# Two encoder layers on one core: a split per conv block, evacuations behind the next block's casts, and projections in two 1024-column chunks

## The chip, the cores and the metric

The kernel runs on one core of one Trainium2 chip. Its time is the device time of one execution in microseconds (us). The time before is the median of three runs. A profiled execution of the same kernel gives the trace; its own time differs a little from that median and stands in the table below.

The engines are named as the profile names them: PE (TensorE, the matrix products; PEld its weight loads), DVE (VectorE), ACT (ScalarE), POOL (GpSimd) and SP (SyncE, which here only issues DMAs).

## The reference, cut to what matters

The input has 256 tokens (two token tiles of 128, called t0 and t1), a model width of 2048 (16 blocks of 128 channels, `kt` 0 to 15) and an inner width of 5632 in the feed-forward part (44 such blocks). There are two layers. Everything is float32.

```python
c_act = jax.nn.silu(c)
for l in range(DEPTH):                       # two layers
    mod = (c_act @ w_mod[l] + b_mod[l]).reshape(bn, 6, d)
    shift_m, scale_m, gate_m = mod[:, 0, None], mod[:, 1, None], mod[:, 2, None]
    shift_f, scale_f, gate_f = mod[:, 3, None], mod[:, 4, None], mod[:, 5, None]

    h = layer_norm(x) * (1.0 + scale_m) + shift_m
    proj = h @ w_in[l]
    uv, q_c, kv_c, k_r, sb, sc, sh, ag = jnp.split(proj, IN_SPLITS, axis=-1)
    y_a = gmlp_mixer(uv, ...)
    y_b = mla_mixer(q_c, kv_c, k_r, ...)
    y_c = short_conv_mixer(sb, sc, sh, ...)
    y_d = conformer_conv(ag, ...)
    y = jnp.concatenate([y_a, y_b, y_c, y_d], axis=-1) @ w_out[l]
    x = layer_norm(ALPHA * x + (1.0 + gate_m) * y, post_mix_g[l], post_mix_b[l])

    h = layer_norm(x) * (1.0 + scale_f) + shift_f
    y = conv_ffn(h, w_up[l], ..., w_down[l])
    x = layer_norm(ALPHA * x + (1.0 + gate_f) * y, post_ffn_g[l], post_ffn_b[l])
```

The weights are read from HBM once each: about 600 MB in the whole run, `w_mod` (the modulation, 2048 x 12288 per layer) among them.

## The kernel before, in words

**Products.** Most products are made of three matrix products in a reduced format: a weight tile `wraw` is split into a rounded part `whi` (a CAST on ACT, L396) and a rest `wlo` (a subtraction on DVE, L397), an activation is split in the same way by `split` (L414: a CAST on ACT at L416, a subtraction on DVE at L417), and PE adds hi x hi, hi x lo and lo x hi. A few products ("exact", tiles `wexact`) take the float32 weight as it is; they need no split, and more time on PE. `splitp` holds four `whi` and four `wlo` tiles of 1024 columns (`wexact` tiles come from the same buffers), and four raw buffers of 1 MB are shared by `wraw`, `wmod` and `gb`. All weight loads are issued by SP in program order, each when its buffer is free.

**The stages**, in order of time: the first input projections of layer 0, done in pieces (`by_pieces`, L1168, fed by `first_mods`, L1428); the rest of the mixers; the output projection, called o0; the up projection with its conv and gate (products `g_c`, `v_c`); the down projection, d0; and the same for layer 1 (o1, d1).

**The modulation** is no stage of its own. A weight unit of 1 MB is loaded (`wmod`) and multiplied and summed along its row by one DVE instruction (L192, or L227 for the gates). `stream` (L338) calls `pump` once per weight unit of the other stages, and a table RATES says how many modulation units that lets in, by stage. What a later step needs and has not been made is made there and then (`need`).

**Stage A, the pieces of layer 0.** A list `turns` sets the order of the pieces: D blocks (the conv branch's columns, one `kt` at a time, four accumulator banks that stay open through the stage) alternate with pieces of U, V, E and B that each take four `kt` at once. Such a piece gets a bank, loads the sum so far into it (`act.copy(o, total)`, L1223), adds its products, and copies the sum out (`act.copy(total, o)`, L1228). Both copies are ACT's. The normalised, modulated activation of one block is `hF`, written by DVE at L1447 when the modulation of that `kt` is known. From `kt` 4 (PLAIN_KT) on, D takes split products and so needs the split activation `hT`. It is made for two blocks at once, after the second block's `hF`:

```python
if kt >= PLAIN_KT and kt % 2 == 1:
    split(hT[kt // 2], hF[kt // 4][:, kt % 4 - 1 : kt % 4 + 1, :])
```

**Output and down projections** (`out_proj`, L601). The 2048 columns are taken in three chunks, of 1024, 512 and 512 columns. A unit of weights is 1 MB: two blocks of 1024 columns, or four of 512, so a unit is always 24 products of 512 columns (or 16 exact ones). Each chunk goes through all blocks (16 for o, 44 for d), with one accumulator bank for each token tile and 512 columns. In o the split activations are kept between chunks; in d there is no room, so each chunk splits all 44 blocks again (instructions `a<-g`, pairs of blocks). When a chunk is done, its banks are evacuated by `finish_bank` (L634): three DVE instructions per bank (`yg` = sum x gate, x update, statistics), queued in `evacs` and popped one per unit of the next chunk. In the last chunk the last four units are held back (`tail`) and done first for t0, then for t1, so that t0's last evacuation and norm (`second`, L667) run while PE still works on t1. t1's last evacuation is ordered behind t0's norm (L641). `gains` loads the norm's gain and bias at the end of the middle chunk.

**Order.** A scheduler places the instructions of each engine, in program order as far as its own cost model likes it; `tc.add_manual_dep(..., order_dep)` pins one instruction behind another of the same engine and adds no wait.

## Time and profile before

| | us |
|---|---|
| median of 3 runs (2260.59 to 2262.27) | 2261.2 |
| profiled execution, its own time | 2257.45 |
| its span, first to last instruction | 2255.7 |
| PE busy | 2198.7 (97%) |
| DVE busy | 1762.5 (78%) |
| ACT busy | 1088.1 (48%) |
| stage A | 0 to about 185 |
| o0 | 307 to 403 |
| d0 | 915 to 1165 |
| o1 | 1411 to 1497 |
| d1 | 2003 to 2244 |

An engine's row of the profile gives its busy time and its share of the span. A row of waits says which instruction group waited for which, the total, how often and the longest. The chain of waits is followed back from the last instruction: each piece is what the next one was released by. A windows row gives, for a stretch, the busy time of PE, PEld, DVE, ACT and POOL with the count of instructions, the granted PE clock, the share of the 16 DMA engines and GB/s. A timeline row gives start, duration, engine, line, operation, output and inputs, and in brackets the idle time ahead of it with what ended it. `L94` is the one line from which all matrix products are issued, so products are told apart by the names of their outputs.

### The profile page before, as it was taken

What the parts mean: (1) busy time and instruction counts of PE and PEld (TensorE: products, weight loads), DVE (VectorE), ACT (ScalarE), POOL (GpSimd) and SP (SyncE); (2) the same over time, 40 slices, a digit from 0 to 9 for tenths busy, and PEclk for the clock granted to TensorE, in tenths of its full rate; (3) what the DMA queues carried; (4) which work ended last, traced back from release to release, by engine and by line L of the source; (5) the groups of instructions that cost most, each with busy time, mean ns of one, the idle gap of its engine ahead of it and who ended that gap; (6) DMA issues with size and microseconds to landing.
All of it is one profiled execution on the core that took longest, in us unless ns stands there. A gap on an engine that the chain in (4) does not pass through costs nothing.

```text
span 2255.7 us, 30853 instructions
## 1 busy us (share of the span) xinstructions
PE 2198.7 (97%) x12128; PEld 1899.5 (84%) x12128; DVE 1762.5 (78%) x2260; ACT 1088.1 (48%) x1617; POOL 28.0 (1%) x49
## 2 busy tenths in 40 slices
PE   7899999899999999999999999999999999999997
PEld 5678886898888888887789899889888888888886
DVE  6779987888888888989876998876765565565676
ACT  4347551454454445544554435444544444454553
POOL 0000000000000000000000000000000000000000
PEclk9999999999999999999999999999999999999999
DMA  9899689687878888898766566765665555555554
GB/s 390 344 370 384 243 337 388 254 313 302 324 290 334 316 333 298 341 348 326 272 240 246 204 226 252 292 227 209 224 255 188 187 187 187 189 195 194 187 188 148
DMA packets 94235, 605.16 MB, mean 268 GB/s; under 512 B 10661, under 2 KB 10853, under 8 KB 28933
## 3 DMA queue, kind: packets, MB, share of 16 engines
q1 hardware_dynamic: 93752, 602.29, 71.7%
q8 instruction: 95, 1.56, 0.3%
q0 software_dynamic: 336, 0.89, 0.1%
q14 instruction: 52, 0.42, 0.0%
HBM read 601.05 MB, written 2.10 MB: 267 GB/s over the span
## 4 chain that ended last, share of the span: by engine, by line
PE 80%; DVE 5%; issue 1%; ACT 1%; DMA 0%; POOL 0%; DVEq 0%; POOLq 0%; ACTq 0%
PE g_c L94 22%; PE v_c L94 22%; PE d L94 19%; PE o L94 7%; PE C_c L94 3%; PE D_c L94 2%; PE U_c L94 1%; DVE wlo L397 1%; PE B_c L94 1%; PE E_c L94 1%; DVE convD L826 1%; DVE wmod L192 0%; PE ps_xT L532 0%; DVE a L417 0%; DMA wraw<-in_w_out_dram 0%
## 5 line engine op out<-in xcount | busy, mean ns | idle before, releaser
L396 ACT CAST whi<-wraw 128x1024 fp32r<-128x1024 f32 (+1 forms) x632 | 644.9, 1044 | 774.0 <-PE g_c L94 209.9
L397 DVE TENSOR_TENSOR wlo<-wraw,whi 128x1024 fp32r<-128x1024 f32 (+1 forms) x632 | 751.6, 1214 | 313.2 <-ACT whi L396 299.4
L94 PE MATMUL d<-whi,a 128*128 128x512 f32 x1344 | 388.2, 390 | 2.0 <-ACT whi L396 2.0
L94 PE MATMUL v_c<-hT,whi 128*128 128x512 f32 (+1 forms) x1456 | 341.5, 383 | 0.0
L94 PE MATMUL g_c<-hT,whi 128*128 128x512 f32 (+1 forms) x1344 | 313.3, 380 | 0.0
L94 PEld LDWEIGHTS v_c<-hT,whi 128*128 128x128 f32 x1456 | 264.6, 189 | 48.0
L192 DVE SCALAR_TENSOR_TENSOR wmod<-wmod,cB 128x2048 f32<-128x2048 f32 x126 | 286.9, 2285 | 17.5 <-DMA wmod<-in_w_mod_turned_dram 17.4
L94 PEld LDWEIGHTS d<-whi,a 128*128 128x128 f32 x1344 | 252.7, 188 | 55.0 <-ACT whi L396 2.8
L94 PEld LDWEIGHTS g_c<-hT,whi 128*128 128x128 f32 x1344 | 243.5, 189 | 43.2
L94 PE MATMUL d<-wlo,a 128*128 128x512 f32 x672 | 234.3, 391 | 4.6 <-DVE wlo L397 4.6
L94 PE MATMUL v_c<-hT,wlo 128*128 128x256 f32 x1400 | 190.2, 283 | 0.0
L94 PEld LDWEIGHTS v_c<-hT,wlo 128*128 128x128 f32 x1400 | 183.1, 191 | 6.5
L94 PE MATMUL g_c<-hT,wlo 128*128 128x256 f32 x1280 | 175.8, 283 | 0.0
L94 PEld LDWEIGHTS g_c<-hT,wlo 128*128 128x128 f32 x1280 | 168.2, 191 | 5.9
L94 PEld LDWEIGHTS d<-wlo,a 128*128 128x128 f32 x672 | 126.5, 188 | 33.8 <-DVE wlo L397 7.6
L227 DVE SCALAR_TENSOR_TENSOR macc<-wmod,cact,macc 128x2048 f32<-128x2048 f32 x60 | 140.7, 2344 | 8.0 <-DMA wmod<-in_w_mod_gates_dram 7.9
L416 ACT CAST a<-g 128x512 fp32r<-128x512 f32 x132 | 80.9, 618 | 72.0 <-PE d L94 70.1
L94 PE MATMUL o<-whi,a 128*128 128x512 f32 x384 | 110.6, 393 | 0.0
L94 PE MATMUL D_c<-hT,whi 128*128 128x256 f32 x432 | 84.6, 296 | 12.1 <-ACT hT L416 11.1
L417 DVE TENSOR_TENSOR a<-g,a 128x512 fp32r<-128x512 f32 x132 | 88.0, 684 | 7.4 <-ACT a L416 7.4
L94 PEld LDWEIGHTS o<-whi,a 128*128 128x128 f32 x384 | 72.0, 188 | 16.3 <-issue 1.2
L94 PEld LDWEIGHTS D_c<-hT,whi 128*128 128x128 f32 x432 | 70.5, 199 | 17.7 <-ACT hT L416 14.4
(345 smaller groups left out, 2525.2 us busy)
## 6 DMA issues: line engine op xcount, KB each, us to landing
wraw<-in_ffn_w_up_dram SPq DMA_DIRECT2D x168, 1024.0 KB, 4.9
wmod<-in_w_mod_turned_dram SPq DMA_DIRECT2D x126, 1024.0 KB, 6.3
wraw<-in_ffn_w_down_dram SPq DMA_DIRECT2D x88, 1024.0 KB, 4.8
wmod<-in_w_mod_gates_dram SPq DMA_DIRECT2D x64, 1024.0 KB, 5.6
wraw<-in_w_in_dram SPq DMA_DIRECT2D x27, 1024.0 KB, 4.9
wraw<-in_w_out_dram SPq DMA_DIRECT2D x26, 1024.0 KB, 6.4
wexact<-in_w_in_dram SPq DMA_DIRECT2D x46, 512.0 KB, 7.8
wexact<-in_ffn_w_up_dram SPq DMA_DIRECT2D x16, 512.0 KB, 8.9
```

What stands on the lines that cost most here:

```text
L94: pe.matmul(o, lhsT, rhs, start=start, stop=stop, skip_group_check=True)
L192: i = dve.scalar_tensor_tensor(out=raw, in0=raw, scalar=1.0, in1=cB[:, k0 : k0 + n], op0=ALU.mult, op1=ALU.mult, accum_out=total)
L227: i = dve.scalar_tensor_tensor(out=acc, in0=w, scalar=col, in1=acc, op0=ALU.mult, op1=ALU.add)
L396: act.copy(hi[:, :m], r)
L397: i = dve.tensor_tensor(out=lo[:, :m], in0=r, in1=hi[:, :m].bitcast(F32), op=ALU.subtract)
L416: act.copy(hi, src)
L417: dve.tensor_tensor(out=lo, in0=src, in1=hi.bitcast(F32), op=ALU.subtract)
L826: dve.scalar_tensor_tensor(out=yd[:, j, 30 - k :], in0=glu[:, j, : S - 30 + k], scalar=CW(k, j), in1=yd[:, j, 30 - k :], op0=ALU.mult, op1 ...
```

## The change

There are four parts, none of which alters what is computed.

1. **Split per block.** `first_mods` splits each block from `kt` 4 on by itself as soon as its `hF` is written, 128 x 256 elements instead of 128 x 512 per instruction, so six pairs become twelve single splits on ACT and on DVE. The CASTs (the activation's, and that of the block's weights) are collected in a table `casts`.
2. **Evacuations behind casts.** In `side`, the copy of a piece's sum out of its bank gets an order dependence behind the CASTs of the next D block, if the next turn is one. The remaining transposes of x are popped at fixed turns.
3. **Two chunks.** Output and down projections take 1024 and 1024 columns. In d each block is split twice instead of three times: 132 `a<-g` instructions become 88 on ACT and on DVE. In o0 six units of the second chunk are exact, as many products as before (eight products of each kind move between two mixers' columns). The tail is done bank by bank for each token tile. The modulation is pumped in the last chunk too, up to five units from its end; the first chunk's gate is fetched ahead of its last products, its evacuations start as each token tile ends, and `gains` runs six units ahead of the end.
4. **Rates.** Layer 0: out 1.3 to 1.53, down 0.83 to 0.7. Layer 1: out 0.6 to 0.65, down 0.7 to 0.6.

Three places show what the instruction order does. First ACT in stage A, around two D blocks (`hT<-hF` and the `whi` behind it are a D block's casts; `sumU<-U` evacuates a piece, `V<-sumV` opens the next). Before:

```order
L1228 COPY sumU<-U_0_650 128x512
L1223 COPY V_0_728<-sumV 128x512
L1228 COPY sumU<-U_1_661 128x512
L1223 COPY V_1_735<-sumV 128x512
L416 CAST hT<-hF_134 128x2x256
L396 CAST whi<-wraw 128x1024
L1228 COPY sumV<-V_0_728 128x512
L1223 COPY E_0_788<-sumE 128x512
```

and now:

```order
L417 CAST hT<-hF_134 128x256
L397 CAST whi<-wraw 128x1024
L1229 COPY sumU<-U_0_640 128x512
L1224 COPY V_0_720<-sumV 128x512
L1229 COPY sumU<-U_1_651 128x512
L1224 COPY V_1_727<-sumV 128x512
L417 CAST hT<-hF_134 128x256
L397 CAST whi<-wraw 128x1024
L1229 COPY sumV<-V_0_720 128x512
```

The casts stood behind both copies of the piece ahead of them; now they stand ahead of both, and every block has its own activation cast.

Second, DVE in d0, before in the second and third chunk (`yg<-d_102400` evacuates the second chunk's bank of t0):

```order
L417 TENSOR_TENSOR a<-g,a 128x2x256 x4
L397 TENSOR_TENSOR wlo<-wraw,whi 128x1024 x2
L192 SCALAR_TENSOR_TENSOR wmod,total<-wmod,cB 128x2048
L417 TENSOR_TENSOR a<-g,a 128x2x256
L205 TENSOR_TENSOR mod_3_12_8698<-total,bcol_104 128x8
L417 TENSOR_TENSOR a<-g,a 128x2x256 x2
L397 TENSOR_TENSOR wlo<-wraw,whi 128x1024 x2
L225 TENSOR_SCALAR macc<-wmod,cact 128x2048
L417 TENSOR_TENSOR a<-g,a 128x2x256
L639 TENSOR_TENSOR yg<-d_102400_8315,gate_5_4778 128x512
```

and now, in the second of two chunks:

```order
L398 TENSOR_TENSOR wlo<-wraw,whi 128x1024 x2
L192 SCALAR_TENSOR_TENSOR wmod,total<-wmod,cB 128x2048
L418 TENSOR_TENSOR a<-g,a 128x2x256
L398 TENSOR_TENSOR wlo<-wraw,whi 128x1024 x2
L418 TENSOR_TENSOR a<-g,a 128x2x256
L192 SCALAR_TENSOR_TENSOR wmod,total<-wmod,cB 128x2048
L398 TENSOR_TENSOR wlo<-wraw,whi 128x1024 x2
L418 TENSOR_TENSOR a<-g,a 128x2x256
L192 SCALAR_TENSOR_TENSOR wmod,total<-wmod,cB 128x2048
L205 TENSOR_TENSOR mod_3_12_8904<-total,bcol_104 128x8
```

Per unit of weights (two `wlo`) there is one `a` in place of two, and the modulation units reach further into the stage.

Third, DVE at the end of d0, where the next stage waits for t0's norm (`x_97` is t0; the rows up to `rs_d0p` are its last evacuation and statistics). Before:

```order
L639 TENSOR_TENSOR yg<-d_153600_8817,gate_5_4778 128x512
L642 SCALAR_TENSOR_TENSOR x_97<-x_97,yg 128x512
L645 BN_STATS st_d_7394<-x_97 128x6
L512 BN_AGGR mv_d0p_9243<-st_d_7394 128x2
L514 TENSOR_SCALAR rs_d0p_9245<-mv_d0p_9243 128x1
```

and now:

```order
L641 TENSOR_TENSOR yg<-d_102400_8310,gate_5_4734 128x512
L641 TENSOR_TENSOR yg<-d_102401_8311,gate_5_4734 128x512
L644 SCALAR_TENSOR_TENSOR x_97<-x_97,yg 128x512 x2
L647 BN_STATS st_d_7406<-x_97 128x6 x2
L514 BN_AGGR mv_d0p_9185<-st_d_7406 128x2
L516 TENSOR_SCALAR rs_d0p_9187<-mv_d0p_9185 128x1
```

Two banks are evacuated ahead of the norm in place of one. The same holds for t1 behind it, and for the ends of o0 and o1. PE's order at these ends has 24 products of t1 for its first bank and 24 for its second behind the last product of t0 in d0, d1 and o1; in o0, where the exact blocks of t1's first bank are mostly done earlier, one exact and 12 split products, and then four exact and 12 split ones.

The diff:

```diff
@@ -33,8 +33,8 @@
 
 
 RATES = [
-    dict(B=1.3, C=1.5, out=1.3, first=1.2, up=0.68, down=0.83),
-    dict(D=0.8, U=0, V=0, B=0.3, C=0.6, E=0.6, out=0.6, up=0.3, down=0.7),
+    dict(B=1.3, C=1.5, out=1.53, first=1.2, up=0.68, down=0.7),
+    dict(D=0.8, U=0, V=0, B=0.3, C=0.6, E=0.6, out=0.65, up=0.3, down=0.6),
 ]
 
@@ -56,9 +56,9 @@
 
 GROUPS = {
     "w_in": ((C_UV, 512), (C_UV + 512, 512), (C_Q, 768), (C_SB, 512), (C_SC, 1024), (C_AG, 1024)),
-    "w_out": ((0, 1024), (1024, 512), (1536, 512)),
+    "w_out": ((0, 1024), (1024, 1024)),
...
-    "ffn_w_down": ((0, 1024), (1024, 512), (1536, 512)),
+    "ffn_w_down": ((0, 1024), (1024, 1024)),
 }
 
 
@@ -356,6 +356,7 @@
             tc.add_manual_dep(i.ins, name, order_dep, reason="the norm is what the next products wait for")
 
     exact_turn = [0]
+    cast = [None]
@@ -393,7 +394,7 @@
                 hi = splitp.tile([P, 1024], F32R, tag="whi", name="whi")
                 lo = splitp.tile([P, 1024], F32R, tag="wlo", name="wlo")
             r = raw[:, k * width : k * width + m]
-            act.copy(hi[:, :m], r)
+            cast[0] = act.copy(hi[:, :m], r)
             i = dve.tensor_tensor(out=lo[:, :m], in0=r, in1=hi[:, :m].bitcast(F32), op=ALU.subtract)
             held(i, "split")
             for j in range(per):
@@ -413,8 +414,9 @@
 
     def split(dst, src):
         hi, lo = dst[:2]
-        act.copy(hi, src)
+        i = act.copy(hi, src)
         dve.tensor_tensor(out=lo, in0=src, in1=hi.bitcast(F32), op=ALU.subtract)
+        return i
 
     def group(w, c0, width, name, then, ntm=0, nk=2, hF=None, bg=0, spare=0, begun=None):
 
@@ -596,7 +598,7 @@
 
         return cps, rest
 
-    CHUNKS = ((0, 1024), (1024, 512), (1536, 512))
+    CHUNKS = ((0, 1024), (1024, 1024))
 
     def out_proj(l, w, src, order, gate_of, name, post_g, post_b, before, then, plain={}, bg=0):
 
@@ -604,25 +606,25 @@
         stats = [new_stats(f"{name}{t}") for t in range(2)]
         box, kept = {}, {}
 
-        def products(t, item, ps, u, nk):
+        def products(t, item, ps, u, nk, banks=None):
...
@@ -726,7 +728,7 @@
             last = c0 + width == D
             nk = 2048 // width
             units = nkt // nk
-            state = {"tail": []}
+            state = {"tail": [], "ps": []}
 
...
@@ -749,42 +751,41 @@
...
-            def unit(item, u, state=state, c0=c0, width=width, nk=nk, last=last, units=units):
-                if u == 0:
-                    state["ps"] = [
-                        [acc_tile(f"{name}_{c0}{t}{i}") for i in range(width // 512)] for t in range(2)
-                    ]
+            def banks_of(t, state=state, c0=c0, width=width):
+                state["ps"].append([acc_tile(f"{name}_{c0}{t}{i}") for i in range(width // 512)])
+
+            def unit(item, u, state=state, c0=c0, nk=nk, last=last, units=units):
                 if last and u >= units - 4:
                     state["tail"].append((item, u))
-                    if evacs:
+                    return
+                if not last and u == units - 1:
+                    box["gate"] = gate_of()
+                for t in range(2):
+                    if u == 0:
+                        banks_of(t)
+                    products(t, item, state["ps"], u, nk)
+                    if not last and u == units - 1:
+                        evacs.extend(lambda t=t, i=i: finish_bank(t, i, state["ps"], c0) for i in range(2))
+                    if last and u == 0 and t == 0:
+                        while len(evacs) > 2:
+                            evacs.pop(0)()
+                if evacs and last and u > 0:
+                    evacs.pop(0)()
+                if last and u == units - 6:
+                    gains()
+
+            for u in range(units):
+                stream(lambda: load(u), lambda item, u=u, unit=unit: unit(item, u), bg, not last or u < units - 5)
+
+            def done(state=state, c0=c0, nk=nk, last=last):
+                if not last:
+                    while len(evacs) > 3:
                         evacs.pop(0)()
                     return
                 for t in range(2):
-                    products(t, item, state["ps"], u, nk)
-                if evacs:
-                    evacs.pop(0)()
-
-            for u in range(units):
-                stream(lambda: load(u), lambda item, u=u, unit=unit: unit(item, u), bg, not last)
-
-            def done(state=state, c0=c0, nk=nk, last=last):
-                if c0 == 0:
-                    box["gate"] = gate_of()
-                if c0 + 512 == D - 512:
-                    gains()
-                for t in range(2):
-                    for item, u in state["tail"]:
-                        products(t, item, state["ps"], u, nk)
-                while evacs:
-                    evacs.pop(0)()
-                if not last:
-                    evacs.extend(
-                        lambda t=t, i=i: finish_bank(t, i, state["ps"], c0)
-                        for t in range(2)
-                        for i in range(len(state["ps"][t]))
-                    )
-                    evacs.pop(0)()
-                    return
+                    for i in range(2):
+                        for item, u in state["tail"]:
+                            products(t, item, state["ps"], u, nk, (i,))
                 if before is not None:
                     before()
                 for t in range(2):
@@ -1216,7 +1217,7 @@
                 else:
                     chan_major([None] * i + [o], kt, part, (2 * i, 2 * i + 1), first, last)
 
-        def side(g, kts):
+        def side(g, kts, before):
             for i, total in enumerate(sums[g]):
                 o = acc_tile(f"{g}{l}_{i}")
                 if kts[0] > 0:
@@ -1225,7 +1226,9 @@
                 if g == "U" and kts[-1] == KT - 1:
                     u_banks.append(o)
                 else:
-                    act.copy(total, o)
+                    i = act.copy(total, o)
+                    for c in before:
+                        tc.add_manual_dep(i.ins, c.ins.name, order_dep, reason="the next conv block is waited for")
...
+                if g == "D" and not exact:
+                    casts[k].append(cast[0])
 
...
-                side(g, kts)
+                g1, k1 = turns[n + 1] if n + 1 < len(turns) else ("", ())
+                side(g, kts, casts.get(k1[0], ()) if g1 == "D" else ())
             if kts[:1] == (LATE_KT,) and g != "D":
                 next(mods)
-            if n > 6 and rest_of_x:
+            if n in (6, 7, 13, 14, 20, 21):
                 rest_of_x.pop(0)()
         mix_v(None, [[x] for x in sums["V"]])
         phase(l, "B")
@@ -1425,6 +1431,8 @@
 
+    casts = {}
+
     def first_mods(hF):
 
         quarter = normed_T(hF)
@@ -1445,8 +1453,8 @@
             x = hF[kt // 4][:, kt % 4, :]
             sc, sh = MOD[(0, SCALE_M, kt)], MOD[(0, SHIFT_M, kt)]
             i = dve.tensor_scalar(out=x, in0=x, scalar1=sc, scalar2=sh, op0=ALU.mult, op1=ALU.add)
-            if kt >= PLAIN_KT and kt % 2 == 1:
-                split(hT[kt // 2], hF[kt // 4][:, kt % 4 - 1 : kt % 4 + 1, :])
+            if kt >= PLAIN_KT:
+                casts[kt] = [split([h[:, kt % 2, :] for h in hT[kt // 2][:2]], x)]
...
-            plain={1024: 2, 1536: 4} if l == 0 else {},
+            plain={1024: 6} if l == 0 else {},
         )
```

More of the change, by code (lines that the diff above doesn't have):

```diff
@@ L611, in products @@
                 sp = (u + 1) * nk == nkt and k == nk - 1
-                n = len(ps[t])
-                cols = [slice(i * 512, (i + 1) * 512) for i in range(n)]
+                banks = banks or range(len(ps[t]))
+                cols = [slice(i * 512, (i + 1) * 512) for i in range(len(ps[t]))]
                 ahi, alo = acts[k]
@@ L616, in products @@
                 if lo is None:
-                    for i in range(n):
+                    for i in banks:
                         mm(ps[t][i], ah, hi[:, cols[i]], st, sp)
                     continue
-                for i in range(n):
+                for i in banks:
                     mm(ps[t][i], ah, hi[:, cols[i]], st, False)
-                for i in range(n):
+                for i in banks:
                     mm(ps[t][i], ah, lo[:, cols[i]], False, False)
                 al = alo[:, t * P : (t + 1) * P]
-                for i in range(n):
+                for i in banks:
                     mm(ps[t][i], al, hi[:, cols[i]], False, sp)
```

## The prediction

> **What bounds the kernel now.** I read the page first, for the share of PE, then what PE waited for, then the stretches in which it waited.
>
> ```profile
> span 2255.7 us, 30853 instructions
> PE 2198.7 (97%) x12128; PEld 1899.5 (84%) x12128; DVE 1762.5 (78%) x2260; ACT 1088.1 (48%) x1617; POOL 28.0 (1%) x49
> ```
>
> PE is busy for all but 57 us of the span, and the change leaves its products as many as they were. So a gain can only come out of those 57 us and out of products that ran at a lower clock. The waits of PE say where they lie:
>
> ```profile
> PE D_c L94 <- ACT hT L416: 11.1, 6, 4.0
> PE ps_xT L532 <- ACT xn L97: 10.0, 4, 5.3
> ...
> PE d L94 <- DVE wlo L397: 4.6, 7, 1.9
> PE d L94 <- ACT whi L396: 2.0, 2, 1.7
> ```
>
> The first row is stage A: the D blocks wait for their split activation. The second is the start of the next stage after a norm. The last two are the down projection. The stretches, with busy time of PE, PEld, DVE, ACT, POOL, then granted clock, DMA share and GB/s:
>
> ```profile
> 60.00:80.00 20.00, 15.86 (x86) 14.35 (x85) 17.05 (x21) 6.67 (x12) 0.00 (x0) 0.83 0.88 333
> 80.00:100.00 20.00, 17.09 (x90) 14.60 (x88) 14.09 (x16) 7.79 (x12) 0.00 (x0) 0.91 0.96 356
> ...
> 186.00:216.00 30.00, 30.00 (x141) 26.41 (x140) 28.68 (x25) 18.29 (x46) 0.39 (x2) 1.00 1.02 413
> ...
> 20.00:186.00 166.00, 151.94 (x805) 126.36 (x806) 116.16 (x132) 75.85 (x123) 4.10 (x7) 0.96 0.93 365
> 307.00:403.00 96.00, 95.92 (x337) 63.09 (x336) 80.61 (x101) 21.71 (x28) 1.60 (x2) 1.00 0.92 352
> 1049.00:1110.00 61.00, 54.43 (x228) 42.13 (x227) 60.21 (x75) 33.54 (x42) 0.00 (x0) 0.99 0.81 297
> 914.60:1164.60 250.00, 243.40 (x1056) 198.19 (x1055) 219.90 (x257) 121.71 (x154) 1.47 (x2) 0.99 0.81 300
> 2002.80:2244.40 241.60, 241.59 (x1065) 199.20 (x1063) 160.89 (x183) 121.91 (x151) 0.92 (x1) 1.00 0.52 184
> ```
>
> In 1049 to 1110, the middle of d0, DVE is busy 60.21 of 61.00 us: there it is the bound. Elsewhere PE is, except in stage A, where no engine is full and the D blocks wait.
>
> **Down projection, layer 0.** The chain of waits gives PE's undisturbed pace:
>
> ```profile
> 914.60 134.68 PE d L94 x594
> ```
>
> 134.68/594 is 0.2267 us per product, so the 1056 products of d0 need 239.4 us; the stretch is 250.0. It loses 10.6 us. What DVE does there per product unit follows from its groups in d0 (914.6 to 1110):
>
> ```profile
> L397 DVE TENSOR_TENSOR wlo<-wraw,whi 128x1024 fp32r<-128x1024 f32 x68 | 80.9, 1220 | 8.6 <-ACT whi L396 7.6
> L192 DVE SCALAR_TENSOR_TENSOR wmod<-wmod,cB 128x2048 f32<-128x2048 f32 x26 | 59.4, 2283 | 0.0
> L417 DVE TENSOR_TENSOR a<-g,a 128x512 fp32r<-128x512 f32 x49 | 32.4, 684 | 4.0 <-ACT a L416 4.0
> ```
>
> A unit of 24 products takes PE 24 x 0.2267 = 5.44 us. In the 512-column chunks DVE had per unit two `wlo` (2.44), two `a` (1.37) and 0.83 modulation units (0.83 x 2.283 = 1.89): 5.70, more than PE. Now it is two `wlo`, one `a` (0.68) and 0.7 units (1.60): 4.72, so 0.72 us per unit are free. The 44 `a` that go are 22 in this stage, 15 us of DVE's 219.9. The number of modulation units pumped in the stage stays (33 x 0.83 = 27.4, 39 x 0.7 = 27.3), and they reach into the end of the last chunk, where DVE had been idle. The cost that stays is the first chunk's evacuation: four banks of three instructions; at the 0.684 of the `a` row of the same width I take 8.2 us, which 0.72 per unit needs 11 units to absorb, while four split tiles hold PE for two units, 10.9 us. So a little may show: I take -9.5 us, between -6 (half of the evacuation shows) and -10.6. Cast of ACT: 22 fewer there, hidden (ACT is busy 121.7 of 250).
>
> d1 has 241.6 us against the same 239.4; at most 2.2 to win. DVE is at 161 there, without modulation; -1, between 0 and -2.2.
>
> **Stage A.** ACT works in order, and the casts stood behind the copies of the piece before. ACT, then DVE, then PE:
>
> ```profile
> 65.24 0.62 ACT L416 CAST hT<-hF 128x512 fp32r<-128x512 f32 x1 [3.45 <-DVE hF L1447]
> ...
> 99.19 0.59 ACT L1228 COPY sumU<-U 128x512 f32<-128x512 f32 x1 [2.25 <-PE U L94]
> 99.81 0.59 ACT L1223 COPY V<-sumV 128x512 f32<-128x512 f32 x1
> 100.33 0.61 ACT L416 CAST hT<-hF 128x512 fp32r<-128x512 f32 x1
> ```
>
> ```profile
> 50.87 0.41 DVE L1447 TENSOR_SCALAR hF<-hF,mod 128x256 f32<-128x256 f32 x1
> ...
> 97.75 0.41 DVE L1447 TENSOR_SCALAR hF<-hF,mod 128x256 f32<-128x256 f32 x1
> ```
>
> ```profile
> 65.91 1.31 PE L94 MATMUL D_c<-hT,whi 128*128 128x256 f32 x2 [3.99 <-ACT hT L416]
> ...
> 84.48 1.92 PE L94 MATMUL D_c<-hT,whi 128*128 128x256 f32 x5 [2.79 <-ACT hT L416]
> ```
>
> The rows show both faults that the change takes up. Block 4 had its `hF` at 51.3, but the cast waited for block 5's and came at 65.24: PE stood 3.99 us. Blocks 8 and 9 had theirs by 98.2, but the cast waited on ACT behind a copy that waits for PE, and came at 100.33. With single splits ahead of the copies these waits (11.1 us over six) can go. The two long ones also lowered the clock: 0.83 of 15.86 busy us and 0.91 of 17.09 are 2.7 and 1.5 us. So the stage can win at most 11.1 + 4.2 = 15.3 us. It will not win all: a faster PE frees buffers earlier, and the loads must follow. The stage moves 166 us x 365 GB/s = 60.6 MB, at 413 (the fullest row) 147 us, so the DMA engines would have to run nearly full throughout to give 15. They also run at 413 right behind, so bytes that come late there cannot be made up. From half of the bound I take -7.5; ends 0 and -15.3. The cost of the twelve half-size casts and subtractions instead of six is covered, ACT being busy 76 of 166 us and DVE 116. The copies now stand behind the casts, which can make a piece's bank free later; that is the last rival.
>
> The Trainium skill, "DMA: Bandwidth & Descriptors", section "Where 436 GB/s comes from", says that for loads from HBM the HBM limit of about 358 GB/s per core binds. By that rule stage A, at 365, has no room, its term is 0 and the time 7.5 us higher. The row of 186 to 216 at 413 disagrees for this core.
>
> **Output projection, layer 0.** The rate 1.53 lets in 11 x 1.53 = 16.8 modulation units instead of 12 x 1.3 = 15.6; SP's order has 11 of them and one more half of exact weights among the first chunk's eight `wraw`, where it had 9. That is 2.5 MB more before the second chunk. At 352 GB/s it is 7.1 us if nothing hides it; the 8% of the 96 us in which the DMA engines were idle are 7.7 us and could hold it. PE was full there, so nothing is won. I take +1, ends 0 and +7.
>
> **The three starts of a next stage.** t0's last evacuation now has two banks, three more DVE instructions: at 0.684 each +2.05 us on the path to the norm. The rows of t0's last `yg` and of the end of its norm, for o0 and for d0:
>
> ```profile
> 392.66 0.69 DVE L639 TENSOR_TENSOR yg<-o,gate 128x512 f32<-128x512 f32 x1 [8.73 <-PE o L94]
> ...
> 397.20 2.29 DVE L192 SCALAR_TENSOR_TENSOR wmod<-wmod,cB 128x2048 f32<-128x2048 f32 x1
> ...
> 407.07 0.16 DVE L700 SCALAR_TENSOR_TENSOR rs_o0r<-m_o,rs_o0r 128x1 f32<-128x1 f32 x1 [0.67 <-POOL rs_o0r L125]
> ```
>
> ```profile
> 1153.73 0.69 DVE L639 TENSOR_TENSOR yg<-d,gate 128x512 f32<-128x512 f32 x1 [2.40 <-PE d L94]
> ...
> 1163.69 0.16 DVE L700 SCALAR_TENSOR_TENSOR rs_d0r<-m_d,rs_d0r 128x1 f32<-128x1 f32 x1 [0.73 <-POOL rs_d0r L125]
> ```
>
> In d0 the path took 10.1 us, and t1's 48 products behind t0 take 10.9, so PE waited almost nothing. With 12.2 it waits: 12.2 - 10.9, about 1 for the cast and transpose, +2.3, and if the idle PE starts at a lower clock, as after the 2.79 us above, +0.5: +2.8, ends +1 and +3.5. In o0 the path took 14.6 us, two modulation units of 2.29 within; PE's last product came 10.2 after t0's (the wait of 5.3 ended about 1 us behind 407.07). Now one unit stands there (-2.3), +2.05, and t1's products after t0's are 24 split ones at 0.2267 and five exact ones at 0.43, 7.6 us in place of 10.2 (+2.6): +2.4, and t1's own evacuation of two banks behind that norm +0.6: +3, ends +1 and +5. The 0.43 is an estimate: o0's 95.92 busy us less 240 split products, over its 96 exact ones. In o1 the wait was about 4 us (the row's total of 10.0 is 5.3 and that, mostly); path 12.2 against 10.9 leaves about 2.5: -1, ends -1.5 and +2. The end of d1 has no such order and stays.
>
> The Trainium skill, "TensorE: Matmul & The Clock Gate", Part 1, says that PE falls to half its clock after an idle window of about 3.4 us. By it a wait of 2.3 us costs no clock and d0's start is 0.5 us cheaper. The row of 80 to 100, at 0.91 behind a wait of 2.79, points the other way here.
>
> **Sum.** -7.5 - 9.5 - 1 + 1 + 3 + 2.8 - 1 = -12.2 us. The profiled execution took 2257.45, so it would take 2245.3; the median of the runs lies 3.75 above that execution, so I forecast 2249.
>
> **Rivals.** (1) The loads set stage A. For it: 0.93 of the DMA engines on average, 0.96 and more from 80. Against: 413 next door, and idle DVE and ACT that wait for PE. Then A gives 0, and o0, whose loads are as late, loses 4 in place of 1 (half-way between its ends): sum -1.7, 2259.5. (2) d0 stays with DVE: the evacuations and modulation units find the split tiles empty, and the backlog moves from the narrow chunks to the second wide one. For it: 4.72 of 5.44 us is 0.87 of DVE even without an evacuation. Then half of d0's gain remains, 4.75 us: 2253.7. (3) Stage A frees itself wholly, clock included, -14: 2242.5. (4) A slower kernel: a copy now waits behind a D block's weight cast, and that for its `wraw`. If the load is late, the bank is free late, the next piece opens late, and PE stands for pieces that had run. There are twelve such blocks; from a mean delay of 0.6 us each it eats the gain of A, from 1.0 us the whole gain (12 against 12.2). At 1.5 us each: 2249 + 18 = 2267. Against it: the casts are the first that the next block needs, and four raw buffers are filled ahead.
>
> **Chances.** Forecast 0.54, (1) 0.18, (2) 0.10, (3) 0.12, (4) 0.06. What differs by less than 0.2%, 4.5 us, is no change. Forecast, (3) and most of (2) are faster; (1) lies at 2259.5, mostly within; (4) is slower, and a little of (1). Faster 0.77, same 0.15, slower 0.08. The range is 2239 to 2261: it holds the forecast, (2), (3) and most of (1). The forecast's own range is 2242 to 2256.
>
> **What would show it.** Right: no wait of D_c for hT above 1 us and stage A ending near 177; d0 within 241 us, with DVE below full in its second chunk; waits of ps_xT of about 6.5 at up0 and 2.5 at both others. Wrong: `wraw` waits on PE in o0; D_c waiting for `whi` or pieces for `sumU`; a stretch of d0 with DVE full.

## The result

The changed kernel takes 2245.15 us (median of four runs, 2243.62 to 2246.46) against 2260.89 (2260.56 to 2262.27): a ratio of 0.9929, 95% interval 0.9912 to 0.9946, 15.7 us less. The forecast was 2249, or 12.2 us less. Each run below is compared with runs of the kernel before on the same chip; the brackets give the ratio of the two times and its 95% interval.

The two profiled executions lie closer together, 2257.45 and 2246.46, 11.0 us. The spans fall into these stages, by the first and last product of each (the ends of the rows are the starts of the next; A ends with B_c's first product, "start" is from the last product of one stage to the first weight product of the next):

| us | before | after | difference |
|---|---|---|---|
| A | 182.15 | 173.92 | -8.2 |
| B and C, to the first product of o0 | 124.70 | 129.47 | +4.8 |
| o0 | 96.08 | 101.02 | +4.9 |
| start of up0 | 7.03 | 6.41 | -0.6 |
| up0 | 504.48 | 504.94 | +0.5 |
| d0 | 250.13 | 239.55 | -10.6 |
| start of layer 1 | 1.46 | 2.82 | +1.4 |
| layer 1's mixers | 242.99 | 243.06 | +0.1 |
| o1 | 88.46 | 88.42 | 0 |
| start of up1, and up1 | 505.21 | 501.50 | -3.7 |
| d1 | 241.70 | 241.83 | +0.1 |
| after the last product | 11.3 | 11.7 | +0.4 |

A second profile of the changed kernel (run after_again, below) has the same rows within 1.7 us, but for o1. That row takes 91.75 us there, with a wait of 2.1 us of PE for a weight load that came late, and a low clock behind it.

**What answers to the lines of before.** The waits of PE after (the first two rows of before were 11.1 and 10.0 us, and d waited 6.6 in all):

```profile
PE ps_xT L534 <- ACT xn L97: 6.2, 3, 4.3
...
PE ps_ss L94 <- ACT sqB L978: 2.6, 1, 2.6
PE o L94 <- ACT whi L397: 2.4, 4, 1.4
PE D_c L94 <- DVE wlo L398: 2.3, 3, 1.2
PE D_c L94 <- ACT whi L397: 1.7, 1, 1.7
```

D_c no longer waits for `hT` at all, nor d for anything. Two rows are new: `ps_ss`, the squares of B, and o, which waits for its split weights. The stretches after:

```profile
20.00:178.00 158.00, 152.46 (x811) 128.03 (x812) 116.77 (x140) 76.49 (x129) 4.21 (x8) 0.96 0.96 382
...
178.00:207.00 29.00, 29.00 (x136) 25.52 (x135) 28.10 (x21) 17.16 (x44) 0.00 (x0) 1.00 1.03 412
207.00:223.00 16.00, 13.44 (x56) 11.29 (x55) 11.63 (x18) 12.85 (x36) 1.02 (x1) 0.79 0.89 365
...
326.00:346.00 20.00, 17.75 (x74) 13.04 (x72) 17.41 (x17) 5.46 (x6) 0.00 (x0) 1.00 1.00 375
...
915.90:1155.30 239.40, 239.40 (x1057) 197.95 (x1055) 205.66 (x232) 110.74 (x131) 1.42 (x2) 1.00 0.83 311
```

Stage A now runs at 382 GB/s, where it was 365. d0 has PE busy for all of its 239.4 us, and DVE has 205.66 us there instead of 219.90. In 207 to 223 PE has a wait and a low clock. In 326 to 346 the DMA engines are full (1.00) and PE is not; before, PE was full in the same part of o0:

```profile
330.00:350.00 20.00, 20.00 (x90) 16.57 (x89) 17.15 (x19) 6.00 (x6) 0.00 (x0) 1.00 0.98 372
```

What o0 waits for shows in the chain:

```profile
327.05 7.34 DMA wmod<-in_w_mod_turned_dram
334.48 2.31 DVE wmod L192 x2
336.81 7.62 DMA wraw<-in_w_out_dram
345.61 1.24 DVE wlo L398
346.89 46.58 PE o L94 x127
```

Before, the chain ran through 312 products of o without a break:

```profile
307.19 85.45 PE o L94 x312
```

Now a modulation unit's load stands ahead of o's weights, and PE waits for these.

### The profile page after: what moved, and what is told of

Read it like the earlier page. It is cut to its first block, busy times and chain, and to the rows that moved or that the text cites. A ratio compares the mean times of both kernels' runs of the same rounds, so it can differ in the third digit from the quotient of the medians.

```text
span 2244.7 us, 30821 instructions
## 1 busy us (share of the span) xinstructions
PE 2200.6 (98%) x12128; PEld 1901.5 (85%) x12128; DVE 1738.9 (77%) x2222; ACT 1067.3 (48%) x1579; POOL 29.6 (1%) x49
## 4 chain that ended last, share of the span: by engine, by line
PE 80%; DVE 4%; DMA 1%; ACT 1%; issue 1%; POOL 0%; DVEq 0%; ACTq 0%; POOLq 0%
PE g_c L94 23%; PE v_c L94 22%; PE d L94 21%; PE o L94 5%; PE C_c L94 2%; PE D_c L94 2%; PE U_c L94 1%; PE B_c L94 1%; PE E_c L94 1%; DVE wlo L398 1%; DMA wraw<-in_w_out_dram 1%; DVE convD L827 1%; PE ps_xT L534 0%; DVE wmod L192 0%; DMA wmod<-in_w_mod_turned_dram 0%
## 5 line engine op out<-in xcount | busy, mean ns | idle before, releaser
L94 PE MATMUL d<-whi,a 128*128 128x512 f32 x1344 | 364.1, 389 | 0.0
L94 PE MATMUL d<-wlo,a 128*128 128x512 f32 x672 | 209.9, 389 | 0.0
L94 PEld LDWEIGHTS d<-wlo,a 128*128 128x128 f32 x672 | 126.2, 188 | 26.2
L1337 DVE SCALAR_TENSOR_TENSOR u<-g,pf,u 128x254 f32<-128x254 f32 (+1 forms) x176 | 73.3, 476 | 0.0
L94 PE MATMUL o<-wlo,a 128*128 128x512 f32 x192 | 63.0, 397 | 0.6 <-DVE wlo L398 0.5
```

Of the source, the lines that this page charges most:

```text
L94: pe.matmul(o, lhsT, rhs, start=start, stop=stop, skip_group_check=True)
L1337: dve.scalar_tensor_tensor(out=u[:, sh:], in0=x[:, : S - sh], scalar=col(k, j), in1=u[:, sh:], op0=ALU.mult, op1=ALU.add)
```

## Stage A, taken apart

**Parts 1 and 2 alone.** The kernel before with

```diff
-            if kt >= PLAIN_KT and kt % 2 == 1:
-                split(hT[kt // 2], hF[kt // 4][:, kt % 4 - 1 : kt % 4 + 1, :])
+            if kt >= PLAIN_KT:
+                casts[kt] = [split([h[:, kt % 2, :] for h in hT[kt // 2][:2]], x)]
...
+                    for c in before:
+                        tc.add_manual_dep(i.ins, c.ins.name, order_dep, reason="the next conv block is waited for")
...
-            if n > 6 and rest_of_x:
+            if n in (6, 7, 13, 14, 20, 21):
```

> The kernel before with the splits per block, the copies behind the casts and the fixed turns of the transposes alone (parts 1 and 2). Theory (the parts add, each in its own stage): the first product of B_c comes about 8 us earlier than before (182.15), the first of o about 3.5 earlier, since half is given back behind B; o0 keeps its 96 us, because the rate and chunks are those of before, d0 its 250. Time 4 to 8 us under before. Rival (the loads set stage A, and what it wins is taken back until o0): within 2 us of before.

Measured: 2254.3 against 2262.05 (ratio 0.9969, 0.9958 to 0.9980), 7.75 us less. B_c starts at 171.70, o at 301.20, o0 takes 96.36, d0 251.5. So the gain is real and partly lasts: against the profile of before it is 10.4 us at B_c and 5.6 at o. The theory holds.

**The change without them.** The diff above, taken back in the changed kernel.

> The changed kernel without parts 1 and 2: stage A as before, the two chunks and the rates as changed. Theory: stage A as before (B_c at 182), o0 at 101 us (its weights wait for the modulation's loads), d0 at 239.5, o1's end 3.7 us cheaper: 8 us under before. Rival (o0 waits for loads only because stage A has come nearer): o0 at 96 to 97, and the time 12 to 13 us under before.

Measured: 2251.87 against 2262.05 (0.9959, 0.9945 to 0.9974), 10.2 us less. B_c starts at 182.93, o0 takes 100.65 and d0 239.55. o0's loss is there without an earlier stage A, as the theory had it. 7.75 and 10.2 make 17.9. The two intervals reach some 2.5 and 3.4 us to each side, so this is not told apart from the 15.7 of both.

**Only the splits.** The changed kernel with the copies free of the casts:

```diff
-                side(g, kts, casts.get(k1[0], ()) if g1 == "D" else ())
+                side(g, kts, ())
```

> The changed kernel without the order of the copies behind the casts; the splits per block stay. Theory (each half of part 1 and 2 takes its own waits): the wait of 4.0 at block 4 and its slow clock stay gone, but the casts of the later blocks stand behind copies again, 5 us over the blocks from 8 on; B_c starts 176 to 180 instead of 173.9, the time 1 to 4 us over the changed kernel, as some of it is given back before o anyway. Rival (the splits alone do it): B_c at 174 to 175 and the same time.

Measured: 2251.94 against 2261.61 (0.9955, 0.9940 to 0.9970). B_c starts at 178.28, between the 173.9 of the changed kernel and the 182 to 183.5 of those without either part. Its waits:

```profile
PE D_c L94 <- ACT whi L397: 7.1, 4, 2.3
```

The cast of the block's weights is still behind the copies, and PE waits for that one now. So the splits (with the fixed turns of the transposes, which stay here) bring less than half, the order the rest. Against its own runs of the kernel before it is 9.7 us less, where the changed kernel was 15.7 less: 6 us lost, more than the 1 to 4 expected. o starts at 309.4, 6 us later than in the changed kernel's profile, so none of it was given back.

**The lengths of A, and of B and C, in all runs.** In the ten profiles with both parts (two of them with another rate for C, two with the conv steps moved as below), B_c starts between 171.1 and 174.4 (mean 172.2); in the three with neither, at 182.2, 182.9 and 183.5. Behind it, B and C take 129.5 to 131.0 (mean 130.0) with both parts, and 124.7, 126.2 and 126.2 with neither. So, by the means, stage A wins 10.6 us and 4.3 go again.

**Where they go.** ACT in the changed kernel, ahead of the squares that PE waits for:

```profile
206.17 4.75 ACT L848 ACTIVATE prodD<-gluD,pm 128x242 f32<-128x242 f32 x12 [1.41 <-DVE convD L849]
210.82 1.43 ACT L978 ACTIVATE sqB<-B_c 128x256 f32<-128x256 f32 x5
```

ACT stands in products of the 31-tap conv, which wait for DVE's sums; B's squares are behind them in order. PE has done B and eight products of C at 208.7 and waits 2.56 us. Soon after, its clock is at half for 6.8 us, which costs half of that, 3.4 us. In the kernel a_down07 (below) this takes 10.2 us and costs 5.1:

```profile
213.00:219.80 6.80, 6.80 (x24) 5.91 (x23) 5.84 (x12) 6.80 (x18) 1.02 (x1) 0.50 1.02 411
208.50:218.70 10.20, 10.07 (x34) 8.90 (x35) 7.83 (x15) 8.54 (x25) 1.79 (x1) 0.50 1.00 407
```

PE's own work, its waits and the low clock together make up the length of B and C. The rows are before, the changed kernel without parts 1 and 2 (its clock is at half for 3.4 us), the changed kernel, and a_down07:

```profile
182.10:306.80 124.70, 123.18 (x597) 105.68 (x597) 112.42 (x134) 75.06 (x173) 2.91 (x5) 1.00 0.83 321
182.90:309.10 126.20, 124.68 (x598) 106.91 (x598) 112.51 (x134) 75.00 (x173) 2.88 (x5) 0.99 0.82 318
173.90:303.40 129.50, 126.55 (x603) 108.94 (x601) 111.64 (x133) 76.05 (x177) 4.36 (x5) 0.97 0.82 314
171.30:302.30 131.00, 128.04 (x601) 110.24 (x600) 111.97 (x133) 76.28 (x177) 5.41 (x5) 0.96 0.81 312
```

PE's busy time less what the low clock costs (0, 1.7, 3.4 and 5.1 us) is 123 us in each of the four. The rest is idle time, 1.5 us in the first two and 3.0 in the last two. By the means over all profiles, waits take 1.4 of the 4.3 us and the clock 2.8. The conv steps were then moved:

```diff
-    dict(B=3, C=2, up=2),
+    dict(B=2, C=3, up=2),
```

> The changed kernel with two background steps of the 31-tap conv per unit in B instead of three, and three instead of two in C, in layer 0. Theory (half of stage A's gain is given back because ACT, in order, stands in conv products that wait for DVE, with the squares of B behind them): the wait of 2.6 us for the squares goes, ps_ss starts within 2 us of C_c's first product, and o starts 2 to 5 us earlier than 303.4; the time 2 to 5 us under the changed kernel. Rival (DVE's work before o is what counts, wherever it stands): o starts at 303 or later, because the conv's end comes later.

Measured: 2244.82 against 2261.61 (0.9924, 0.9909 to 0.9939), the changed kernel's time. The wait falls to 1.7 us in three pieces, and B and C together still take 129.65. o starts at 300.76, but B_c started at 171.12: the difference is stage A's. So where the conv steps stand moves the wait and not the sum, as the rival said. That DVE's work sets the sum, as the rival had it, does not show. The row of B and C:

```profile
171.10:300.80 129.70, 127.50 (x603) 108.71 (x601) 110.29 (x132) 76.50 (x177) 3.17 (x5) 0.97 0.79 306
```

PE waits 2.2 us in all instead of 3.0, its clock is at half for 6.8 us as in the changed kernel, and its own time is 0.9 us longer. Why this last part grew is open.

## The down projection, taken apart

**The change with the old rate.**

```diff
-    dict(B=1.3, C=1.5, out=1.53, first=1.2, up=0.68, down=0.7),
+    dict(B=1.3, C=1.5, out=1.53, first=1.2, up=0.68, down=0.83),
```

> The changed kernel with layer 0's rate for the down projection back at 0.83. Theory (d0's gain is the missing split of each unit): DVE has 2.44 + 0.68 + 1.89 = 5.01 us per unit of 5.44, d0 takes 239.4 to 242 and the time is that of the changed kernel within 2 us. Rival (the lower rate made the gain): d0 at 245 or more, and 5 us or more over the changed kernel.

Measured: 2251.2 against 2262.05 (0.9959, 0.9944 to 0.9974). d0 takes 242.5 us, and the wait behind it is 3.7 us instead of 1.2. Of the 3 us more, 1.7 are lost early in the second chunk and the rest near d0's end. The profile is of the slowest of the four executions, 2255.4 us. With two wide chunks the pump has 39 turns in d0 where it had 33, so the old rate makes more there: the trace has 31 modulation units in d0 instead of 26, and DVE is busy 214.2 us instead of 205.7. The expectation missed: the splits do not do it all with these units added.

**The old chunks with the new rate**, one number in the kernel before:

```diff
-    dict(B=1.3, C=1.5, out=1.3, first=1.2, up=0.68, down=0.83),
+    dict(B=1.3, C=1.5, out=1.3, first=1.2, up=0.68, down=0.7),
```

> The kernel before with layer 0's rate for the down projection at 0.7 and nothing else. Run down083 gave d0 242.5 us instead of 239.5, and 1.6 us more of the wait behind it, so the rate has a share. Theory (both are needed: a unit of the narrow chunks still costs DVE 2.44 + 1.37 + 1.60 = 5.41 of 5.44 us, with nothing free for evacuations): d0 between 244 and 248 us, and the 4.3 modulation units that are not made there come later; 2 to 6 us under before. Rival (the rate alone does it): d0 at 241 or less and 9 us or more under before.

Measured: 2248.44 against 2261.61 (0.9941, 0.9926 to 0.9956), 13.2 us less. d0 takes 240.1 us. The rival was right. The theory, which took over the prediction's time per unit, was wrong. The 13.2 are of the medians; between the two profiles it is 9.0 us, of which d0 makes 10.0 and layer 1's mixers 2.5, while the other stages take 3.5 back. The stretches of d0 in this kernel:

```profile
1037.50:1052.00 14.50, 14.50 (x66) 12.01 (x65) 14.50 (x16) 7.98 (x11) 0.00 (x0) 1.00 0.80 307
1052.00:1098.00 46.00, 46.00 (x205) 38.09 (x204) 45.89 (x56) 25.75 (x34) 0.00 (x0) 1.00 0.85 314
...
sum 240.20, PE 239.89 PEld 197.99 DVE 210.45 ACT 121.48 POOL 1.47; mean PE 59.97 PEld 49.50 DVE 52.61 ACT 30.37 POOL 0.37
```

DVE is full for 60 us (60.39 of 60.50), and PE is full beside it: here a full DVE does not yet cost anything. In d0 DVE has 210.45 us of work, 9.5 less than before, and PE's loss fell by 10.0. What is left of it, 0.6 us, lies at d0's very start and not in the narrow chunks.

The stretch behaves much like a ledger: what DVE cannot finish in time is PE's loss. Against the shortest d0, 239.55 us, DVE's work and PE's loss are 219.9 and 10.6 us (before; 1.7 of them are 3.4 us at a clock of 0.51), 214.2 and 3.0 (the old rate in wide chunks), 210.4 and 0.6 (here), 205.7 and 0 (the changed kernel). So a us taken from DVE gives about one back until the loss is gone. Losses at the two ends of d0 do not follow it: split_only, with the changed kernel's code for d0, loses 1.4 us near its end at 205.6 us of DVE. Either remedy clears it: the four fewer modulation units here (9.5 us), or, with 26 units as before, the 22 fewer splits of the changed kernel (14.2 us).

## The output projection, taken apart

**The change with the old rate for o0.**

```diff
-    dict(B=1.3, C=1.5, out=1.53, first=1.2, up=0.68, down=0.7),
+    dict(B=1.3, C=1.5, out=1.3, first=1.2, up=0.68, down=0.7),
```

> The changed kernel with layer 0's rate for the output projection back at 1.3. Theory (o0 waits because the rate puts more modulation loads between its weights): o0 falls from 101 to 97 us, but 2 or 3 modulation units more stand in t0's norm or behind it, 2.3 us each, so the wait for up0's first transpose grows from 4.3 to 7 to 9: the time within 3 us of the changed kernel. Rival (the moved half of exact weights, or the order, does it): o0 stays at 100 or more, and the time is 3 to 5 us over the changed kernel.

Measured: 2251.33 against 2262.05 (0.9954, 0.9937 to 0.9970). o0 takes 96.5 us, so it was the rate that starved it, at the same chunks and exact blocks. The wait at up0 grew to 9.6 us:

```profile
PE ps_xT L534 <- ACT xn L97: 14.1, 4, 9.6
```

4.6 us won in o0, 5.3 lost at the start of up0: no difference there. The time is still 5 to 6 us above the changed kernel by the medians, and 4.7 of them have a place that neither theory nor rival named: at the end of o1 DVE evacuates t0's two banks together, and the wait at up1 is 3.6 instead of 0.65 us.

**Units moved to C.**

```diff
-    dict(B=1.3, C=1.5, out=1.53, first=1.2, up=0.68, down=0.7),
+    dict(B=1.3, C=1.9, out=1.2, first=1.2, up=0.68, down=0.7),
```

> The changed kernel with layer 0's rate for C at 1.9 instead of 1.5 and for the output projection at 1.2 instead of 1.53, so that some 3 modulation units move from o0, where the DMA engines are full, to C, where they are at 0.77. Theory (o0 loses 4 to 5 us to loads): o0 takes 96 to 97 us instead of 101, the wait for up0's first transpose stays at 4 to 6, the time 3 to 5 us under the changed kernel. Rival (DVE is full in C): o starts 3 us or more later than 303.4, and the time is that of the changed kernel or more.

Measured: 2251.16 against 2261.61 (0.9954, 0.9938 to 0.9971). o0 starts at 302.3 and takes 102.6 us. It does not wait for loads; it waits 3.9 us for one split:

```profile
301.07 2.28 DVE L192 SCALAR_TENSOR_TENSOR wmod<-wmod,cB 128x2048 f32<-128x2048 f32 x1
303.29 0.08 DVE L192 DVE_READ_ACCUMULATOR wmod<-wmod,cB 128x1 f32 x1
303.29 1.28 DVE L1135 TENSOR_TENSOR chC<-C_c,sc 128x512 f32<-128x512 f32 x2
304.55 3.25 DVE L1145 SCALAR_TENSOR_TENSOR yc<-chC,pm,yc 128x254 f32<-128x254 f32 x8
307.71 1.29 DVE L1157 TENSOR_TENSOR yc<-yc,sumE 128x512 f32<-128x512 f32 x2
308.92 1.22 DVE L398 TENSOR_TENSOR wlo<-wraw,whi 128x1024 fp32r<-128x1024 f32 x1
```

A modulation unit stands ahead of C's last mix, and o0's split behind both. The rival's reason was right, its place was not: C was not late, o0 was. Behind the wait PE's clock is lower too (0.93 over 302 to 326).

## A version that beats both

**Parts 1 and 2 and the one rate**, with the old chunks and the old rate for o0: the kernel of the first experiment with `down=0.7`.

> The kernel before with parts 1 and 2 and layer 0's rate for the down projection at 0.7: three chunks as before, the rate of o0 as before. Theory (the rate takes d0's 10 us on its own, and stage A's part adds to it): B_c at 171 to 174, o0 at 96 us, d0 at 240, time 19 to 22 us under before, and 3 to 6 under the changed kernel on the same chip, because o0 keeps its pace. Rival (what stage A wins is taken back later when d0 is no longer the slow stage): 13 to 15 us under before, as with the rate alone.

**The changed kernel beside it, on the same chip.**

> The changed kernel again, beside the others on one chip. Theory: 15 to 17 us under before; stage lengths as in its first profile, o0 at 101 us, the wait at up1's first transpose under 1 us.

Measured: 2241.87 against 2260.85 (0.9914, 0.9900 to 0.9927), 19.0 us less, and the changed kernel 2245.63 (0.9932, 0.9920 to 0.9945), 15.2 less. Their runs do not overlap (2240.19 to 2242.08, and 2243.83 to 2247.42). o0 takes 96.4 us here, d0 239.6:

```profile
302.30:398.70 96.40, 96.40 (x338) 63.19 (x336) 81.65 (x101) 21.72 (x28) 1.60 (x2) 1.00 0.90 349
910.50:1150.10 239.60, 239.60 (x1058) 198.14 (x1057) 210.43 (x247) 121.39 (x155) 1.48 (x2) 1.00 0.79 292
```

Run after_again came out as expected but for o1, with a wait of 0.7 us at up1. So the parts nearly add: 7.75 of stage A and 13.2 of the rate are 20.9, and 19.0 came. What the changed kernel has beside them (the two wide chunks with their evacuations, and the other rates) costs 3.8 us net; which of them costs it was not taken apart further.

**With the conv steps moved.**

> The same as a_down07, and in layer 0 two conv steps per unit in B and three in C. Run b2c3 had B and C together at 129.7 us, as without it. Theory (the place of the conv steps moves the wait, not the sum): within 2 us of a_down07. Rival (the wait for the squares costs its 2.6 us): 2.5 us or more under a_down07.

Measured: 2243.03 (0.9918, 0.9904 to 0.9931), not under a_down07. B and C take 129.5, as in b2c3 (131.0 in a_down07).

**With C at 1.7.**

> The same as a_down07, and layer 0's rate for C at 1.7 instead of 1.5, so that one or two of the modulation units that stood in t0's norm at the end of o0 are made in C, whose DMA engines are at 0.75. Theory (those two units are 4.6 us of the 5.3 that PE waits there): the wait falls below 3 us, and the time 2 to 4 us under a_down07's 2241.9. Rival (DVE at the end of C has no room, as with 1.9, where o0 stood 3.9 us for a split): o0 gains a wait of 1 to 4 us at its start, and the time is the same or more.

Measured: 2244.79 against 2261.35 (0.9934, 0.9920 to 0.9948; runs from 2240.61 to 2248.76), not faster than a_down07. The profile is of the fastest of the five executions. The wait at up0 fell from 5.3 to 0.8 us as the theory had it, and o0 went from 96.4 to 100.4 as the rival had it.

```profile
302.00:326.00 24.00, 23.04 (x100) 18.24 (x99) 23.99 (x31) 10.34 (x15) 0.60 (x1) 1.00 0.89 340
326.00:346.00 20.00, 18.09 (x77) 14.04 (x77) 18.16 (x18) 6.00 (x6) 0.00 (x0) 1.00 0.94 369
```

DVE is full in the first 24 us of o0 and PE falls behind there and in the next 20. What the start of up0 wins, o0 loses.

## Why the prediction was right, and where it was not

The time lies in the range and near the forecast, and d0 and stage A carry it as forecast. But several terms of the sum were off, and met in the middle. Of the signs that were named for a wrong forecast, three came in a small form: o waits for its weights, D_c waits 1.7 us for `whi`, and DVE is full in a stretch of d0 (below). With the means over the profiles for A, B and C, the ledger is -10.6 + 4.3 (A, then B and C), +4.6 (o0, mean of two), -0.6 (up0), -10.6 (d0), +1.2 (layer 1, mean of two) and -3.7 (up1): -15.4. It leaves out the rows under 0.5 us, which add up to +1, and the late load in o1. That it comes within 0.3 us of the 15.7 of the medians is partly luck. The single trace of before was quicker than its runs' median, and in B and C quicker (124.7) than two kernels with the same code there (126.2).

**Stage A, -7.5: right in cause, small in size.** The waits of 11.1 us are gone. It won 10.6, of a bound of 15.3, between the forecast and rival (3) with its 14. Part of the bound is left: D_c waits 4.0 us for its weights' splits in the changed kernel, and the clock is 0.83 from 80 to 100:

```profile
80.00:100.00 20.00, 19.26 (x103) 17.47 (x104) 14.37 (x18) 6.64 (x11) 0.00 (x0) 0.83 1.01 389
```

Rival (1), the loads, falls: A now runs at 382 GB/s. The rule in the Trainium skill, "DMA: Bandwidth & Descriptors", section "Where 436 GB/s comes from", that about 358 binds, does not hold for this core: it moved 412 in B, for 29 us. Rival (4) falls too: D_c waits 1.7 us once for its weights' cast, and no piece waits for a bank.

**B and C: a term that was missing.** The forecast let an earlier stage A pass through the next two stages undiminished. It put nothing for PE's wait behind ACT's conv products at the squares of B, nor for the low clock there. 4.3 us went, 1.4 in waits and 2.8 in the clock.

**d0, -9.5: right in size (-10.6) and, for this change, in cause.** DVE was the bound, and 22 fewer splits with as many modulation units freed it. The step that does not hold is the price per unit: it sets 5.70 of DVE in a narrow unit against PE's 5.44, and so makes the gain hang on the narrow chunks going. Run before_down07 has 5.41 in them, almost nothing free for evacuations, and PE loses nothing there. What counts is DVE's backlog over a longer stretch, and the one rate clears it without the wide chunks. Rival (2) falls: no row of d waits. But DVE is full at the start of the second chunk, where the forecast had it below full; PE is full beside it:

```profile
1035.60:1060.00 24.40, 24.40 (x110) 20.20 (x109) 24.40 (x29) 12.10 (x14) 0.00 (x0) 1.00 0.87 326
```

At the old rate (down083) rival (2)'s mechanism shows, with 1.7 us lost in the second wide chunk.

**o0, +1: under-sized.** The price of 7.1 us if nothing hides it was nearer than the idle 8% of the DMA engines that was to hide it; 4.9 were measured (4.3 in the second profile). The idle share was an average over 96 us, and the extra loads came in the 20 us where the engines' share was 0.98 already (330 to 350, above).

**The starts.** up0 +3, measured -0.6: the step that failed took t0's last product as the start of the path, 7.6 us ahead of PE's end. But t0's first bank is done earlier; its evacuation and the modulation unit ran from 10.9 us ahead:

```profile
393.49 0.69 DVE L641 TENSOR_TENSOR yg<-o,gate 128x512 f32<-128x512 f32 x1 [6.60 <-PE o L94]
394.22 0.69 DVE L644 SCALAR_TENSOR_TENSOR x<-x,yg 128x512 f32<-128x512 f32 x1
394.83 2.28 DVE L192 SCALAR_TENSOR_TENSOR wmod<-wmod,cB 128x2048 f32<-128x2048 f32 x1
...
397.71 0.68 DVE L641 TENSOR_TENSOR yg<-o,gate 128x512 f32<-128x512 f32 x1
```

Layer 1's start, +2.8: measured +1.4. The two banks ended together there, the path took 11.8 us of the 12.2 forecast, and PE waited 1.2. up1, -1: measured -3.7, for the reason of up0: t0's first bank was evacuated 2 us before the second, so only one bank stood behind the last product:

```profile
1477.19 0.69 DVE L641 TENSOR_TENSOR yg<-o,gate 128x512 f32<-128x512 f32 x1 [1.65 <-PE o L94]
...
1479.25 0.68 DVE L641 TENSOR_TENSOR yg<-o,gate 128x512 f32<-128x512 f32 x1
```

This hung on the order that came out for o1, and not on the code of o1 alone. In out13 and c19out12, with the same code for o1 but other rates in layer 0, both banks are evacuated together and PE waits 3.6 us. The row is out13's:

```profile
1481.30 1.37 DVE L641 TENSOR_TENSOR yg<-o,gate 128x512 f32<-128x512 f32 x2 [3.00 <-PE o L94]
```

Nothing in the forecast's working chose between the two orders, so the larger gain here was luck.

**d1, -1: nothing.** Of the 2.3 us over the floor, 1.8 are eight other products of PE, which make the first chunk's gate (`ps_gate`).

## What to carry to other kernels

A stage's length is worth taking apart into PE's own work, its waits and its low clock: in B and C the clock cost twice what the waits did. Where one engine is full for a while, price the stretch as a ledger: the work it must do against the time that the other engine leaves it. Two remedies that take work from the same full engine do not add, and the cheaper one (here a rate, one number) may do all of it. A background stream that is moved from one stage to the next takes its price along: of the three rates tried here for o0 and C, two won at one end of o0 about what they lost at the other (out13 and a_down07_c17), and one lost at both (c19out12). What comes earlier in one stage should be followed to the queues of the next before it is booked.

## What the runs showed of the hardware

The granted clock fell after waits shorter than the two that the forecast read (3.99 and 2.79 us). After 2.56 us at the squares of B it was 0.50 for 6.8 us (213.0 to 219.8, above). After 1.2 us at layer 1's start:

```profile
1155.30:1164.00 8.70, 7.19 (x47) 6.74 (x47) 8.54 (x16) 5.82 (x12) 0.98 (x2) 0.80 0.94 341
```

32 products took 5.44 us there, where the next 32 took 3.74. The Trainium skill, "TensorE: Matmul & The Clock Gate", Part 1, gives an idle window of about 3.4 us for this. The rows go lower, at places where PE had transposes or small products around the wait. The run without parts 1 and 2 (no_a) shows that the clock can fall where the profile has no wait. There PE was busy throughout at the squares of B, with 20 products of one column among its work, and the clock fell behind them all the same (0.50 for 3.4 us):

```profile
217.00:238.00 21.00, 21.00 (x99) 17.91 (x98) 18.15 (x25) 17.15 (x45) 1.01 (x1) 0.92 0.79 311
221.90:225.30 3.40, 3.40 (x9) 2.66 (x9) 2.46 (x6) 3.40 (x11) 0.79 (x1) 0.50 1.00 402
```

In the profile of before the same place, with the same products, kept a clock of 1.00. So B and C took 124.7 us there and 126.2 in two other kernels with the same code for these stages. One profile alone does not give a stage to better than that.
